# First attention of a hybrid encoder layer: which keys share a transposed tile

## The chip, the cores and the metric

The kernel runs on one core of a Trainium2 chip. The metric is the device time of one execution in microseconds; smaller is better. Its engines are TensorE (PE; PEld is its loading of weights), VectorE (DVE), ScalarE (ACT), GpSimd (POOL) and SyncE (SP, which issues DMAs). Each works off its own queue in order.

## What is computed

One layer of an encoder over 2048 tokens of width 1024, all in float32: a norm and a projection to queries, keys, values and gates, two attentions side by side, a gated merge, and a feed-forward part. The change is in the first attention:

```
windowed_gqa: 8 query heads, 2 key/value heads (4 query heads share one), head width 64
for each block of 128 tokens i:
    keys  = tokens (i-1)*128 .. (i+2)*128          # 384, fewer at the ends
    sc    = q k^T / 8 - slope(head) * |t - s|
    sc    = -inf where |t - s| > 128 or s is no token
    p     = softmax([sc, sink(head)])[..., :-1]
    y     = p v
```

A query attends to the 128 tokens on either side and to itself, so a row of the 384 keys holds 257 that count.

## The kernel before

**The work in order.** The kernel first makes the projection of the first 1024 tokens, then runs the first attention (function `attn_a`, L763), then the second (`attn_b`, L929), both with the rest of the projection between them as dense work, then the gated merge and the feed-forward part. The framework lays out every engine's queue ahead of time: it takes the instructions in the order in which the program issues them as their priority and places each when a simulated timeline says that it can run.

**The dense work.** `feature_tile` (L207) makes 24 products of 512 columns (L203 to L205) from the projection's weights, which GpSimd and ScalarE split into a high and a low part (L179, L180). `paced` (L838) issues such a piece behind the last product of an earlier attention block, at a fixed rate of pieces to blocks, so TensorE has other work to do while a block's softmax runs.

**One block of the first attention.** There are 2 groups of 4 heads and 16 blocks of 128 tokens in each, so 32 calls of `attn_a(g, i)`. The 128 queries are cut into four parts u of 32 tokens; the 128 rows of a tile are 4 heads x 32 tokens. Part u needs the 288 keys from 32u to 32u + 288 of the block's 384.

- First half: a DMA brings the queries, GpSimd reorders them (L774), TensorE multiplies by the keys (L784, two products a part, of high and low parts), VectorE adds distances and takes the maximum (L786), ScalarE the exponentials (L791), VectorE sums and reciprocals (L792, L793), GpSimd scales (L795). The result s is a tile of 128 x 4 x 384 in which what lies outside a part's 288 keys was set to zero once (L753). There are four such tiles, used in turn.
- Second half, for each of the block's key groups c of 128 keys (three; two at the ends): four transposes, one a part, into one bank of 512 columns (L802); ScalarE copies it to `ph` (L805), rounded to the high part; VectorE subtracts that from the bank to get the low part `pl` (L806); two products, v rows by `ph` (L807) and by `pl` (L808), 512 columns each, add up in one bank over all c. A column of v holds the high and the low part of the 64 values side by side, so the bank has 128 rows; L813 and L814 add its two halves, and a DMA stores the result.

The transposes have two banks to use (tag `pt`), the sums have one (`av`), `ph` and `pl` three buffers each.

**What orders the blocks.** `drive` (L828) issues the first half of a block two blocks ahead of the second half of the one that it then finishes. After the last block the pools of the first attention are closed (L885), and those of the second take the same memory (L889, L890): the left ones are piled up from the bottom of a partition, the right ones down from its top. A tile that takes the place of another can be written when the other was used for the last time. The second attention's units are made alike: a query tile for each of three units in turn (`qb0`, `qb1`, `qb2`, loaded at L934), scores (L947), transposes (L975), copies and subtractions (L980, L981), products (L987).

Of the kernel before, what the change touches and what calls it, by code (L numbers as in the profile page):

```python
# [8 lines left out]
F32 = mybir.dt.float32  # L9
F32R = mybir.dt.float32r  # L10
AF = mybir.ActivationFunctionType
ALU = mybir.AluOpType
# [10 lines left out]
P = 128  # L23
# [72 lines left out]
def encoder_layer(ctx, tc, x, norm_mix, w_in, b_gate, sink, rpb, w_pa, w_pb, w_out,  # L96
                  norm_mlp, w_up, w_down, norm_final, dist_a, mask_b, out):
    nc = tc.nc
    V, A, G, PE, SY = nc.vector, nc.scalar, nc.gpsimd, nc.tensor, nc.sync

    def pool(name, side=None, space=None, stack=None):
        kw = {"reuse_waits": "tile"} if space is not DRAM else {}
        if side:
            kw["side"] = side
        if space:
            kw["space"] = space
        return (stack or ctx).enter_context(tc.tile_pool(name=name, bufs=1, **kw))
# [13 lines left out]
    def psum(tag, bufs):  # L121
        n_ps[0] += 1
        return pps[tag].tile([P, 512], F32, tag=tag, bufs=bufs, name=f"{tag}_{n_ps[0]}")
# [3 lines left out]
    def T(pl, shape, dt, tag, bufs):  # L127
        n_t[0] += 1
        pl = pl[tag] if isinstance(pl, dict) else pl
        return pl.tile(shape, dt, tag=tag, bufs=bufs, name=f"{tag}_{n_t[0]}")  # L130


    ident = cp.tile([P, P], F32, name="ident")
# [37 lines left out]
    def put(dst, src):  # L171
        pending.append((dst, src))

    def flush(keep=0, queue=A):
        while len(pending) > keep:
            queue.dma_start(*pending.pop(0))
# [131 lines left out]
    def ring(stack, tag, shape, dt, bufs, side="right"):  # L308

        pl = pool(f"r_{tag}", side=side, stack=stack)  # L310
        return lambda: T(pl, shape, dt, tag, bufs)
# [263 lines left out]
    for p in range(2):  # L575
        t = T(xp, [P, D], F32, "xin", 8).rearrange("p (k c) -> p k c", k=4)
        c = QUADS[2][0]
# [93 lines left out]
    s_h = ExitStack()  # L671
    hpl = [pool(f"hT{n}", side="left", stack=s_h) for n in range(4)]
    s_a = ExitStack()
    ap_ = pools(s_a, "left", ("ka1", "va1", "qraw", "qa", "sta", "sa", "ya", "ph", "pl", "biasa1", "byhead"), "a")
    ap_.update(pools(s_a, "right", ("biasa0", "va0", "ka0"), "a"))
    hp = {}

# [53 lines left out]
    for h in range(4):  # L731
        at = slice(h * A_Q, (h + 1) * A_Q)
# [4 lines left out]
    def make_bias_a(g):  # L737
        t = T(ap_, [P, A_K], F32, f"biasa{g}", 1)
        SY.dma_start(t, dist_a)
        G.tensor_scalar(t, t, slope[:, g : g + 1], 1.0, ALU.mult, ALU.mult)  # L740
        bias_a[g] = t
# [4 lines left out]
    vas = [T(ap_, [P, 16, P], F32R, f"va{g}", 1) for g in range(2)]  # L746
# [8 lines left out]
    def load_kv(g, m, behind=None):  # L755
        k, kd = kas[g][:, :, m * (S // 2) : (m + 1) * (S // 2)], ks_a[m][g]
        with tc.issue_after(behind) if behind else nullcontext():
# [2 lines left out]
            SY.dma_start(k[64:128, 1].bitcast(F32), kd[0:64])  # L760
            SY.dma_start(vas[g][:, 8 * m : 8 * m + 8].bitcast(F32), vs_a[m][g])

    def attn_a(g, i):  # L763
        c0, c1 = (1 if i == 0 else 0), (2 if i == 15 else 3)
        if bias_a[g] is None:

            with tc.issue_after(shares[2]):
                make_bias_a(g)
        base = (i - 1) * P
        by_head = T(ap_, [P, 4, P], F32, "qraw", 3)  # L770
        q = T(ap_, [P, 4, 4, A_Q], F32R, "qa", 2)
        s = sas[len(began) % 4]
        began.append(SY.dma_start(by_head, qs_a[g][i // 8][:, :, i % 8]).ins)
        G.tensor_copy(out=q.rearrange("p u h q -> p h u q"), in_=by_head.rearrange("p h (u q) -> p h u q", u=4))  # L774
        ka, v = kas[g], vas[g]
        st = T(ap_, [P, 8, 4], F32, "sta", 8)
        mx, nm, sm, es, ri = (st[:, k, :] for k in range(5))
        sink_g = sink_p[:, g : g + 1]
        span = [(max(u * A_Q, c0 * P), min(u * A_Q + A_K, c1 * P)) for u in range(4)]
        for u, (lo, hi) in enumerate(span):  # L780
            n = hi - lo
            ps = psum("s", 3)
            for z in range(2):
                PE.matmul(ps[:, :n], q[:, u].rearrange("p h q -> p (h q)"), ka[:, z, base + lo : base + hi],  # L784
                          start=z == 0, stop=z == 1)
            V.tensor_tensor_reduce(out=s[:, u, lo:hi], in0=ps[:, :n], in1=bias_a[g][:, lo - u * A_Q : hi - u * A_Q],  # L786
                                   scale=1.0, scalar=sink_g, op0=ALU.add, op1=ALU.max, accum_out=mx[:, u : u + 1])
        A.activation(nm, mx, AF.Copy, scale=-1.0)
        A.activation(es, mx, AF.Exp, bias=sink_g, scale=-1.0)
        for u, (lo, hi) in enumerate(span):  # L790
            A.activation(s[:, u, lo:hi], s[:, u, lo:hi], AF.Exp, bias=nm[:, u : u + 1], accum_out=sm[:, u : u + 1])  # L791
        V.tensor_tensor(out=sm, in0=sm, in1=es, op=ALU.add)  # L792
        V.reciprocal(ri, sm)  # L793
        for u, (lo, hi) in enumerate(span):
            share = G.tensor_scalar(s[:, u, lo:hi], s[:, u, lo:hi], ri[:, u : u + 1], 1.0, ALU.mult, ALU.mult)  # L795
        shares.append(share.ins)
        yield
        po = psum("av", 1)
        for c in range(c0, c1):
            pt = psum("pt", 2)  # L800
            for u in range(4):
                PE.transpose(pt[:, u * P : (u + 1) * P], s[:, u, c * P : (c + 1) * P], ident)  # L802
            ph = T(ap_, [P, 512], F32R, "ph", 3)
            pl = T(ap_, [P, 512], F32R, "pl", 3)
            A.copy(ph, pt)  # L805
            V.tensor_tensor(out=pl, in0=pt, in1=ph.bitcast(F32), op=ALU.subtract)  # L806
            PE.matmul(po, v[:, i - 1 + c, :], ph, start=c == c0, stop=False)  # L807
            last = PE.matmul(po, v[:, i - 1 + c, :], pl, start=False, stop=c == c1 - 1).ins  # L808
        done.append(last)
        t = T(ap_, [64, 512], F32, "ya", 2)  # L810
        t4 = t.rearrange("d (h u q) -> d h u q", h=4, u=4)
        by_u = po.rearrange("p (u h q) -> p h u q", u=4, h=4)
        A.copy(t4, by_u[64:128])  # L813
        V.tensor_tensor(out=t4, in0=by_u[0:64], in1=t4, op=ALU.add)  # L814
        flush(queue=SY)
        put(y_a[g].rearrange("(h d) t -> d h t", d=64)[:, :, i * P : (i + 1) * P],
            t.rearrange("d (h q) -> d h q", h=4))
# [56 lines left out]
    for g in (1, 0):  # L874
        load_kv(g, 0)
    drive((attn_a(g, i) for g in (1, 0) for i in range(7)), live, False)
    paced(fill, range(12), 24, 3)
    flush(queue=SY)
    for g in range(2):
        load_kv(g, 1, began[8 + 3 * g])  # L880
    drive((attn_a(g, i) for g in range(2) for i in range(7, 16)), live, True)
    paced(fill, range(12, 24), 24, 3)
    del done[:]
# [579 lines left out]
    rows = [ring(s_dn, tag, [P, BT], F32, 8) for tag in "XYZW"]  # L1463
# [120 lines left out]
    for n in (1, 6, 2, 7, 5, 3, 4):  # L1584
        for group in ((range(8),) if n != 4 else (range(4), range(4, 8))):
# [14 lines left out]
            last = []  # L1600
# [55 lines left out]
```

## Time and profile before

| | |
|---|---|
| median of 3 runs | 2606.74 us (2605.96 to 2606.89) |
| the profiled execution | 2605.6 us, span of its instructions 2603.8 us |
| TensorE busy | 2571.4 us, 99% of the span |
| VectorE, ScalarE, GpSimd busy | 1608.0, 1232.4, 368.1 us |
| the first attention | about 376 to 646 us of the span |
| the second attention | about 610 to 1021 us |

A row of a group gives line, engine, operation, the tiles written and read, the shape and the count; then the busy time, the mean duration in ns of one, and the idle time of the engine before them, with what ended it. A row of a timeline gives the start and the duration in us. "SPq" is the queue that issues DMAs. A row of busy times by stretch gives the length of the stretch and then, engine by engine, the busy time and the number of instructions, then TensorE's granted clock, the DMA share and GB/s.

### The profile page before, as it was taken

What the parts mean: (1) busy time and instruction counts of PE and PEld (TensorE: products, weight loads), DVE (VectorE), ACT (ScalarE), POOL (GpSimd) and SP (SyncE); (2) the same over time, 40 slices, a digit from 0 to 9 for tenths busy, and PEclk for the clock granted to TensorE, in tenths of its full rate; (3) what the DMA queues carried; (4) which work ended last, traced back from release to release, by engine and by line L of the source; (5) the groups of instructions that cost most, each with busy time, mean ns of one, the idle gap of its engine ahead of it and who ended that gap; (6) DMA issues with size and microseconds to landing.
All of it is one profiled execution on the core that took longest, in us unless ns stands there. A gap on an engine that the chain in (4) does not pass through costs nothing.

```text
span 2603.8 us, 34627 instructions
## 1 busy us (share of the span) xinstructions
PE 2571.4 (99%) x12140; PEld 2143.3 (82%) x12140; DVE 1608.0 (62%) x2621; ACT 1232.4 (47%) x2261; POOL 368.1 (14%) x493
## 2 busy tenths in 40 slices
PE   8999999999999999999999999999999999999999
PEld 6888788788888888888888888888888888888887
DVE  8865666665544444665478677766656535554766
ACT  5334356666555555542335544644444322323454
POOL 1000124444655541000000000100000000000010
PEclk9999999999999999999999999999999999999999
DMA  5657486465975745865466665854428825445555
GB/s 185 203 155 202 132 260 166 119 167 154 247 212 173 207 140 188 273 202 161 143 198 207 238 222 200 306 173 146 158 100 313 290 97 186 146 148 167 186 193 171
DMA packets 354127, 490.40 MB, mean 188 GB/s; under 512 B 28808, under 2 KB 188808, under 8 KB 351776
## 3 DMA queue, kind: packets, MB, share of 16 engines
q1 hardware_dynamic: 346896, 471.14, 57.6%
q10 hardware_dynamic: 7056, 17.04, 1.8%
q8 instruction: 96, 1.57, 0.2%
q14 instruction: 79, 0.65, 0.1%
HBM read 328.64 MB, written 159.45 MB: 187 GB/s over the span
## 4 chain that ended last, share of the span: by engine, by line
PE 90%; DVE 4%; DMA 2%; ACT 2%; issue 1%; SPq 0%; POOL 0%; DVEq 0%; POOLq 0%; ACTq 0%
PE b L300 15%; PE b L302 15%; PE b L301 15%; PE mm L203 6%; PE mm L205 6%; PE mm L204 6%; PE zb L300 3%; PE zb L302 3%; PE zb L301 3%; PE pt L203 2%; PE pt L204 2%; PE pt L205 2%; PE av L987 2%; PE pt L975 2%; PE s L947 2%; PE pt L802 1%
## 5 line engine op out<-in xcount | busy, mean ns | idle before, releaser
L301 PE MATMUL b<-dwh,dah 128*128 128x512 f32 x896 | 348.5, 389 | 0.0
L302 PE MATMUL b<-dwh,dah 128*128 128x512 f32 x896 | 347.6, 389 | 0.0
L300 PE MATMUL b<-dwh,dah 128*128 128x512 f32 x896 | 339.6, 389 | 0.0
L296 ACT CAST dah<-da 128x1024 fp32r<-128x1024 f32 (+1 forms) x128 | 120.9, 945 | 368.0 <-PE b L302 245.9
L297 DVE TENSOR_TENSOR dah<-da,dah 128x1024 fp32r<-128x1024 f32 (+1 forms) x128 | 139.5, 1090 | 221.3 <-ACT dah L296 216.8
L301 PE MATMUL b<-ubh,uwhlb 128*128 128x512 f32 x592 | 230.3, 389 | 0.0
L300 PE MATMUL b<-ubh,uwhlb 128*128 128x512 f32 x592 | 230.2, 389 | 0.0
L302 PE MATMUL b<-ubh,uwhlb 128*128 128x512 f32 x592 | 229.2, 389 | 0.0
L203 PE MATMUL mm<-hT,whl 128*128 128x512 f32 x544 | 218.6, 402 | 0.0
L205 PE MATMUL mm<-hT,whl 128*128 128x512 f32 x544 | 215.2, 396 | 0.0
L204 PE MATMUL mm<-hT,whl 128*128 128x512 f32 x544 | 214.4, 394 | 0.0
L301 PEld LDWEIGHTS b<-dwh,dah 128*128 128x128 f32 x896 | 168.2, 188 | 35.0
L302 PEld LDWEIGHTS b<-dwh,dah 128*128 128x128 f32 x896 | 168.2, 188 | 34.9
L300 PEld LDWEIGHTS b<-dwh,dah 128*128 128x128 f32 x896 | 168.2, 188 | 34.9
L300 PE MATMUL zb<-zh,zwhl 128*128 128x512 f32 x476 | 186.7, 394 | 8.3 <-DVE zc L293 3.5
L301 PE MATMUL zb<-zh,zwhl 128*128 128x512 f32 x476 | 186.5, 392 | 0.0
L302 PE MATMUL zb<-zh,zwhl 128*128 128x512 f32 x476 | 183.5, 392 | 0.3 <-DVE zwhl L297 0.3
L293 DVE TENSOR_TENSOR uc<-b,uc 128x512 f32<-128x512 f32 x160 | 109.1, 689 | 105.0 <-PE b L302 104.0
L1526 POOL TENSOR_TENSOR st<-st,power 128x1 f32<-128x1 f32 x16 | 13.4, 841 | 925.2 <-DVE st L1525 925.2
L300 PEld LDWEIGHTS b<-ubh,uwhlb 128*128 128x128 f32 x592 | 111.1, 188 | 23.4 <-issue 0.4
L301 PEld LDWEIGHTS b<-ubh,uwhlb 128*128 128x128 f32 x592 | 111.1, 188 | 23.2
L302 PEld LDWEIGHTS b<-ubh,uwhlb 128*128 128x128 f32 x592 | 111.1, 188 | 23.1
(254 smaller groups left out, 5839.3 us busy)
## 6 DMA issues: line engine op xcount, KB each, us to landing
at<-uc SPq DMA_DIRECT2D x224, 256.0 KB
da<-at SPq DMA_DIRECT2D x96, 512.0 KB
dw<-in_w_down_dram SPq DMA_DIRECT2D x160, 256.0 KB
uraw<-in_w_up_dram SPq DMA_DIRECT2D x32, 1024.0 KB
raw<-in_w_in_dram SPq DMA_DIRECT2D x34, 512.0 KB
zraw<-in_w_in_dram SPq DMA_DIRECT2D x16, 1024.0 KB
z<-zg SPq DMA_DIRECT2D x64, 256.0 KB
qraw<-qs_a SPq DMA_DIRECT2D x32, 256.0 KB
```

What stands on the lines that cost most here:

```text
L203: PE.matmul(ps, lh, rh, start=first, stop=False)
L204: PE.matmul(ps, lh, rl, start=False, stop=False)
L205: PE.matmul(ps, ll, rh, start=False, stop=last)
L293: return eng.tensor_tensor(out=out, in0=a, in1=b, op=op).ins
L296: A.copy(hi, src)
L297: return eng.tensor_tensor(out=lo, in0=src, in1=hi.bitcast(F32), op=ALU.subtract).ins
L300: PE.matmul(ps, lh, rh, start=first, stop=False, skip_group_check=True)
L301: PE.matmul(ps, lh, rl, start=False, stop=False, skip_group_check=True)
L302: PE.matmul(ps, ll, rh, start=False, stop=last, skip_group_check=True)
L947: PE.matmul(ps[:, :n], q[:, i, :], kv[:, z, B_R0[i] // 4 : (B_R0[i] + B_NR[i]) // 4, 4 * B_C0[j] : 4 * (B_C0[j] + w)], start=z == 0, stop= ...
L975: PE.transpose(pt[:kp, at + (i - i0) * P : at + (i - i0 + 1) * P], s[i][:, rr : rr + kp], ident)
L987: last = PE.matmul(po[:, i0 * P : (i0 + ni) * P], v[:kp, c, :], src[:kp, o : o + ni * P], start=first, stop=(c == 7 and z == 1), skip_grou ...
```

## The change

The second half of a block takes its keys in another grouping. Of the outer groups c = 0 and c = 2, parts 0 and 1 have all or most of their keys in c = 0 and up to 64 in c = 2, and parts 2 and 3 the other way round.

- `whole` is called twice: for the middle group (c = 1, all four parts), and for the outer ones (c = 0 for parts 0 and 1, c = 2 for parts 2 and 3), four transposes, a copy and a subtraction each. The first gives two products of 512 columns, the second four of 256 (two v row groups, high and low).
- `halved` takes the rests: 64 keys of c = 2 for parts 0 and 1, 64 of c = 0 for parts 2 and 3. Its four transposes have 64 columns of s and give 64 rows. The high part goes to rows 0 to 63 of `ph`, the low part to rows 64 to 127 of the same tile. A product with v rows that are doubled does both at once: two products of 256 columns.
- The doubled rows stand in a new tile `ve` (two buffers). GpSimd fills it in the first half of a block, right behind the reordering of the queries, by up to four copies of 64 rows by 128.
- `halved` is transposed first; its products come last. All products of a block are issued behind all of its transposes.
- `pl` has two buffers in place of three; `ve` is the last pool of the left pile.

A block at the ends has one rest in place of two and half of the outer group.

```diff
-    ap_ = pools(s_a, "left", (..., "ph", "pl", "biasa1", "byhead"), "a")
+    ap_ = pools(s_a, "left", (..., "ph", "pl", "biasa1", "byhead", "ve"), "a")
...
+    def v_rows(g, k, c):
+        return vas[g][64 - 32 * c : 128 - 32 * c, k]
...
         G.tensor_copy(out=q..., in_=by_head...)
+        ve = T(ap_, [P, 2, P], F32R, "ve", 2)
+        for c in (0, 2):
+            if c0 <= c < c1:
+                rows = v_rows(g, i - 1 + c, c)
+                for half in (slice(0, 64), slice(64, P)):
+                    G.tensor_copy(out=ve[half, c // 2], in_=rows)
...
         po = psum("av", 1)
-        for c in range(c0, c1):
+        todo = []
+
+        def whole(keys):
             pt = psum("pt", 2)
-            for u in range(4):
+            for u, c in keys:
                 PE.transpose(pt[:, u * P : (u + 1) * P], s[:, u, c * P : (c + 1) * P], ident)
+            at = slice(keys[0][0] * P, (keys[-1][0] + 1) * P)
             ph = T(ap_, [P, 512], F32R, "ph", 3)
-            pl = T(ap_, [P, 512], F32R, "pl", 3)
-            A.copy(ph, pt)
-            V.tensor_tensor(out=pl, in0=pt, in1=ph.bitcast(F32), op=ALU.subtract)
-            PE.matmul(po, v[:, i - 1 + c, :], ph, start=c == c0, stop=False)
-            last = PE.matmul(po, v[:, i - 1 + c, :], pl, start=False, stop=c == c1 - 1).ins
+            pl = T(ap_, [P, 512], F32R, "pl", 2)
+            A.copy(ph[:, at], pt[:, at])
+            V.tensor_tensor(out=pl[:, at], in0=pt[:, at], in1=ph[:, at].bitcast(F32), op=ALU.subtract)
+            for c in sorted({c for _, c in keys}):
+                us = [u for u, cc in keys if cc == c]
+                cs = slice(us[0] * P, (us[-1] + 1) * P)
+                todo.extend((v[:, i - 1 + c, :], t[:, cs], cs) for t in (ph, pl))
+
+        def halved(cs):
+            pt = psum("pt", 2)
+            ph = T(ap_, [P, 512], F32R, "ph", 3)
+            at = slice(0 if 2 in cs else 256, 512 if 0 in cs else 256)
+            for c in cs:
+                for u in (0, 1) if c == 2 else (2, 3):
+                    k = 2 * P if c == 2 else 64
+                    PE.transpose(pt[0:64, u * P : (u + 1) * P], s[:, u, k : k + 64], ident)
+            A.copy(ph[0:64, at], pt[0:64, at])
+            V.tensor_tensor(out=ph[64:P, at], in0=pt[0:64, at], in1=ph[0:64, at].bitcast(F32), op=ALU.subtract)
+            for c in cs:
+                at = slice(0, 256) if c == 2 else slice(256, 512)
+                todo.append((ve[:, c // 2], ph[:, at], at))
+
+        halved([c for c in (2, 0) if c0 <= c < c1])
+        stacked = todo[:]
+        del todo[:]
+        whole([(u, 1) for u in range(4)])
+        whole([(u, 2 * (u // 2)) for u in range(4) if c0 <= 2 * (u // 2) < c1])
+        todo += stacked
+        for n, (rows, p, at) in enumerate(todo):
+            last = PE.matmul(po[:, at], rows, p, start=n == 0, stop=n == len(todo) - 1, skip_group_check=True).ins
         done.append(last)
```

More of the change, by code (lines that the diff above doesn't have):

```diff
@@ L673, in encoder_layer @@
     s_a = ExitStack()
-    ap_ = pools(s_a, "left", ("ka1", "va1", "qraw", "qa", "sta", "sa", "ya", "ph", "pl", "biasa1", "byhead"), "a")
+    ap_ = pools(s_a, "left", ("ka1", "va1", "qraw", "qa", "sta", "sa", "ya", "ph", "pl", "biasa1", "byhead", "ve"), "a")
     ap_.update(pools(s_a, "right", ("biasa0", "va0", "ka0"), "a"))
```

## The prediction

> **What bounds the kernel now.** I read the page first: the line of engines, then the chain that ended last.
>
> ```profile
> span 2603.8 us, 34627 instructions
> ...
> PE 2571.4 (99%) x12140; PEld 2143.3 (82%) x12140; DVE 1608.0 (62%) x2621; ACT 1232.4 (47%) x2261; POOL 368.1 (14%) x493
> ...
> PE 90%; DVE 4%; DMA 2%; ACT 2%; issue 1%; SPq 0%; POOL 0%; DVEq 0%; POOLq 0%; ACTq 0%
> ```
>
> TensorE is busy for 99% of the span and is 90% of the chain. What shortens its own work counts in full; what shortens another engine's counts only where TensorE waits for it. Next I read the busy times of the first attention's stretch, from the first transpose of L802 to the last product of L808, with the columns PE, PEld, DVE, ACT, POOL.
>
> ```profile
> 376.00:646.00 270.00, 264.21 (x1432) 220.23 (x1431) 166.94 (x475) 179.10 (x497) 124.45 (x191) 1.00 0.58 157
> ```
>
> TensorE stands idle for 5.8 of the 270 us, at the full granted clock (1.00). The others have room: VectorE 62%, ScalarE 66%, GpSimd 46%. The same stretch by groups:
>
> ```profile
> L806 DVE TENSOR_TENSOR pl<-pt,ph 128x512 fp32r<-128x512 f32 x92 | 62.8, 688 | 18.4 <-ACT ph L805 17.9
> ...
> L802 PE MATMUL pt<-ident,sa 128*128 128x128 f32 x368 | 55.9, 272 | 2.5 <-DVE pl L806 2.3 <-DVE sta L793 0.2
> L805 ACT CAST ph<-pt 128x512 fp32r<-128x512 f32 x92 | 53.1, 585 | 51.6 <-PE pt L802 50.8
> ...
> L808 PE MATMUL av<-pl,va 128*128 128x512 f32 x92 | 38.0, 413 | 1.8 <-DVE pl L806 1.4
> L807 PE MATMUL av<-ph,va 128*128 128x512 f32 x92 | 37.9, 412 | 0.3 <-DVE ya L814 0.3
> ...
> L180 POOL TENSOR_TENSOR whl<-raw,whl 128x1024 fp32r<-128x1024 f32 x13 | 31.2, 2396 | 14.5 <-ACT whl L179 12.5 <-PE s L784 1.5 <-PE pt L802 0.6
> ```
>
> The 92 rounds are 28 inner blocks with three key groups and 4 edge blocks with two: 28 x 3 + 4 x 2. Each round is four transposes, a copy, a subtraction and two products 512 wide.
>
> **What one product costs TensorE.** A matmul's duration (412 ns) isn't its price, because matmuls overlap; the step from start to start is. I read it from the timeline of TensorE. The eleven rows left out first are all 512 wide.
>
> ```profile
> 502.19 0.40 PE L204 MATMUL mm<-hT,whl 128*128 128x512 f32 x1
> ...
> 504.96 0.39 PE L204 MATMUL mm<-hT,whl 128*128 128x512 f32 x1
> ...
> 505.92 0.60 PE L802 MATMUL pt<-ident,sa 128*128 128x128 f32 x4
> 506.27 0.48 PE L204 MATMUL mm<-hT,whl 128*128 128x512 f32 x1
> 506.58 0.40 PE L205 MATMUL mm<-hT,whl 128*128 128x512 f32 x1
> ```
>
> Twelve steps in 2.77 us: 0.231 us for 512 columns. From 505.92 to 506.58 stand four transposes and one such product: (0.66 - 0.231) / 4 = 0.107 us for a transpose. Products 256 wide, and transposes of 96 columns, are in the second attention:
>
> ```profile
> 690.59 0.33 PE L987 MATMUL av<-phb,vb 128*128 128x256 f32 x1
> 690.75 0.28 PE L987 MATMUL av<-plb,vb 128*128 128x256 f32 x1
> 690.87 0.28 PE L987 MATMUL av<-phb,vb 128*128 128x256 f32 x1
> 690.99 0.28 PE L987 MATMUL av<-plb,vb 128*128 128x256 f32 x1
> 691.11 0.49 PE L975 MATMUL pt<-ident,sb 128*128 128x128 f32 x3
> ...
> 693.81 0.38 PE L975 MATMUL pt<-ident,sb 128*96 128x128 f32 x2
> ```
>
> Four steps in 0.52 us: 0.13 us each, three of them 0.12. I take 0.13, since in the new order too a change of width comes just before; 0.12 is the other end. Two 96-column transposes end 0.38 us after the first starts; one alone takes 0.27, so the step is 0.11: fewer stationary columns don't shorten it.
>
> **The change, part by part.**
>
> *Products.* An inner block had 6 of 512 columns. It now has 2 of 512 and 6 of 256: four for the outer key groups, whose halves are joined in one tile, and two for the stacked rests, which need no second pass for the low parts. An edge block goes from 4 of 512 to 2 of 512 and 3 of 256. Inner: 4 x 0.231 - 6 x 0.13 = 0.144 us saved; edge: 2 x 0.231 - 3 x 0.13 = 0.072. Sum: 28 x 0.144 + 4 x 0.072 = 4.3 us (6.1 by 0.12). It all lies on the engine that bounds.
>
> *Transposes.* There are 12 and 8 a block, as before, but 4 (edge: 2) have 64 columns, together 120. No row shows 64. Below, the 96-column step says nothing is gained or lost: 0. Above, if each ran alone, it would cost its record, 0.272, in place of 0.107: 120 x 0.165 = 19.8 us. I take 0, since 96 columns is the nearest row.
>
> *Copies and subtractions.* Three of each in an inner block before and after; the stacked pair is 64 partitions by 512 columns, and time doesn't follow partitions: the 64x512 subtraction L814 is as long as L806.
>
> ```profile
> L814 DVE TENSOR_TENSOR ya<-av,ya 64x512 f32<-64x512 f32 x31 | 21.1, 680 | 7.7 <-ACT ya L813 7.5
> ```
>
> An edge block gets a third pair, but two of its three are half as wide: 4 extra instructions on each engine, under 1 us for all, beside TensorE. The gain on these engines is none, whatever becomes of the "two tiles".
>
> *Doubled v rows.* 120 new GpSimd copies of 64 partitions x 128 elements. The nearest rows, one far smaller and one four times as wide:
>
> ```profile
> L774 POOL CAST qa<-qraw 128x512 fp32r<-128x512 f32 x32 | 19.6, 615 | 53.9 <-issue 40.0 <-PE s L784 5.2 <-DMA qraw<-qs_a 3.2
> ...
> L735 POOL COPY byhead<-sink_t 32x2 f32<-32x2 f32 x4 | 0.7, 179 | 0.1
> ```
>
> On the line between them, 128 elements cost 0.179 + 126 x (0.436 / 510) = 0.29 us; ends 0.18 and 0.62. 120 x 0.29 = 35 us (21 to 74), so GpSimd goes from 124 to about 160 of 265 us. Hidden by the dense matmuls that fill TensorE's queue; 1.2 us a block stands in GpSimd's queue behind the cast L774 and ahead of the scalings L795. If the cover is gone, that is rival 2.
>
> *Order.* The stacked rests are transposed first and multiplied last, and all products stand behind all transposes. What stalls TensorE now:
>
> ```profile
> DVE sa L786 <- PE pt L802: 15.9, 15, 3.1
> ...
> PEld av L808 <- DVE pl L806: 5.1, 13, 0.8
> ```
>
> Low-part products wait 5.1 us in 13 of 92 places. Of the new ones only the 32 outer rounds follow their subtraction closely: the middle round's has the outer transposes in between, and the stacked one's both rounds. At best 60 of 92 places go: 3.3 us. At worst none, since the third round needs a bank that the first subtraction must free, as now. I take 1.0, nearer to none.
>
> *Handover.* By the pool lists, the new tile "ve" lies on top of the left pile, where the second attention's second query tile, qb1, comes to lie. Before, qb1 lay on biasa1:
>
> ```profile
> L786 DVE CUSTOM_DVE_ANT_0 sa<-s,biasa,byhead x128: 384/512/540, 371.5 to 607.0; 128x288 f32<-128x288 f32 x112, 128x160 f32<-128x160 f32 x4, 128x192 f32<-128x192 f32 x4, 128x224 f32<-128x224 f32 x4
> ```
>
> ```profile
> 607.89 0.57 SPq L934 DMA_DIRECT2D qb<-qs_b  x1
> ```
>
> ```profile
> 645.91 0.39 PE L808 MATMUL av<-pl,va 128*128 128x512 f32 x1
> ...
> 652.46 1.44 PE L947 MATMUL s<-kb,qb 128*128 128x384 f32 x6
> ```
>
> Its load went out 0.4 us after the last use of that bias. Now it must wait for the last stacked product, which stands where 645.91 stands: 38 us later. What is queued behind it on SP then is the next unit's loads, and the scores of that unit, 8 products, come about as much later. I price this at nothing: the next unit's scores wait until 652.46 anyway, and dense pieces fill the gap. Rival 3 has it otherwise.
>
> *Sum.* -4.3 - 1.0 = -5.3 us, against the profiled execution's 2605.6 (span 2603.8 and 1.8 around it): 2600.3. The median of the runs shown is 1.1 above that execution, so 2606.7 - 5.3 = **2601.4**.
>
> **The rivals.**
>
> [...]
>
> 2. *GpSimd's queue holds the scores back.* Scores now run up to four blocks ahead: L786 waits for L802 (15.9 us above) because there are four score tiles. "ve" has two buffers, so its copies for block n wait for the last product of block n-2, and behind them in GpSimd's queue stand the scalings of n, the cast of n+1 and now and then a weight split (2.4 us, 13 times). The lead shrinks to about two blocks. If TensorE then stalls 1 us at each of 13 splits: -5.3 + 13 = +7.7, **2614.4**. Against it: GpSimd is half idle, and two blocks are 2 x 270 / 32 = 17 us.
>
> 3. *The gain is not passed on.* The chain goes from the first attention into a transfer:
>
> ```profile
> 653.87 10.75 DMA kb<-ks_b
> ```
>
> If the late qb1 or this load sets when the second attention gets going, TensorE idles for what it saved: **2606.7**, give or take 2. Against it: in this stretch TensorE had dense work and hardly waited.
>
> **How the numbers follow.** Forecast 0.45, rival 1 0.25, rival 2 0.15, rival 3 0.15. A measurement of this kernel tells about 0.2%, 5.2 us, from no change. The forecast's own range is 2597 to 2605 (0.12 us products and 3.3 us of stalls gone, to 0.13 with some of the stalls back), so it is faster by more than 5.2 us in 0.27 and within in 0.18. Rival 1, 2606 to 2617 by how much of 0.16 us is laid bare: same 0.10, slower 0.15. Rival 2: same 0.02, slower 0.13. Rival 3: faster 0.01, same 0.11, slower 0.03. Together faster 0.28, same 0.41, slower 0.31. The range 2597 to 2614 leaves out the upper ends of rivals 1 and 2, some 0.13, and 0.03 below; transposes that each run alone would be at the very top of it and beyond.
>
> **What would show it.** Right: L802's steps stay 0.11 with 64 columns; 64 products of 512 and 180 of 256 columns at 0.12 to 0.13; 120 GpSimd copies near 0.29 us; TensorE idle in the stretch at or below 5.8 us; the last product some 5 us before 645.9; everything after it shifted by that. [...] Rival 2: long waits of GpSimd's copy for the products, and TensorE waiting for L795 or L774. Rival 3: an earlier end of the stretch and idle time of TensorE behind it. Wrong would be the whole argument if another stage of the schedule moves: spans before 376 us or after 1016 us that differ by more than a microsecond.

## The result, and the profile after

The changed kernel takes **2618.2 us** (median of 6 runs, 2617.6 to 2619.0), against 2607.2 for the kernel before in the same runs (6 runs, 2606.0 to 2609.0): 1.0042 times as long, with a 95% interval of 1.0032 to 1.0052. It is slower by 11 us. The forecast was 2601.4 us, the range 2597 to 2614.

Three lines from the head of the page of the changed kernel: the span, the engines' busy times, the chain that ended last.

```profile
span 2617.2 us, 34925 instructions
...
PE 2576.6 (98%) x12200; PEld 2150.7 (82%) x12200; DVE 1613.7 (62%) x2625; ACT 1233.4 (47%) x2265; POOL 401.5 (15%) x613
...
PE 92%; DVE 3%; DMA 2%; ACT 1%; issue 1%; SPq 0%; POOL 0%; DVEq 0%; POOLq 0%; ACTq 0%
```

TensorE is *busy* 5.2 us longer (2571.4 before), though it has less to do. That is the first thing to explain. The first attention's stretch, now to its last product at 657.9 us (columns as in the prediction), has TensorE idle for 9.5 us, against 5.8, and the mean granted clock is 0.99, no longer 1.00:

```profile
376.00:657.90 281.90, 272.42 (x1527) 230.02 (x1526) 172.02 (x478) 181.23 (x503) 155.20 (x300) 0.99 0.57 153
```

The groups that the change made, between 376 and 660 us (busy time, mean ns; then the idle time before them):

```profile
L831 PE MATMUL pt<-ident,sa 128*64 128x128 f32 x120 | 19.8, 282 | 0.0
...
L845 PE MATMUL av<-ph,va 128*128 128x512 f32 x32 | 13.7, 430 | 2.2 <-ACT ph L817 1.8
L845 PE MATMUL av<-ph,ve 128*128 128x256 f32 x60 | 12.8, 291 | 0.0
```

TensorE is never idle before the 64-column transposes (L831). What one costs is seen in the timeline of TensorE:

```profile
504.17 0.28 PE L845 MATMUL av<-pl,va 128*128 128x256 f32 x1
504.29 0.27 PE L845 MATMUL av<-ph,va 128*128 128x256 f32 x1
504.40 0.28 PE L845 MATMUL av<-pl,va 128*128 128x256 f32 x1
504.52 0.41 PE L845 MATMUL av<-ph,ve 128*128 128x256 f32 x2
504.76 0.60 PE L813 MATMUL pt<-ident,sa 128*128 128x128 f32 x4
505.12 0.48 PE L203 MATMUL mm<-hT,whl 128*128 128x512 f32 x1
...
511.92 0.60 PE L831 MATMUL pt<-ident,sa 128*64 128x128 f32 x4
512.27 0.52 PE L793 MATMUL s<-ka,qa 128*128 128x288 f32 x2
```

A product of 256 columns is stepped past in 0.12 us (504.17, 504.29, 504.40, 504.52). Four transposes of 64 columns take 0.35 us from the start of the first to the next instruction (511.92 to 512.27), four of 128 columns 0.36 (504.76 to 505.12). Over all groups of four with a score product right behind them, between 360 and 700 us, the median is 0.355 us with 64 columns (17 groups, after) and 0.354 with 128 (21 groups, before); the product ahead is stepped past in 0.23 us and the score product behind in 0.22, with either width. So a switch between the two widths shows no cost.

**Where the time went.** I call "the stretch" what lies between the first dense product (L203, at 360.7 us before) and the last (at 1027.9). In it both attentions run. I add up a fixed step for every TensorE instruction by its width (0.228 us for 512 columns, in proportion for narrower ones, 0.06 for the second attention's products of 128 columns, 0.109 for a transpose): that is its *work*, an estimate from the steps in the timelines. A second part is time at half clock, which I come to below. The rest is what these two leave over: waits above all, most of them too short to show as idle time, since the records of neighbouring products overlap (idle by the records: 7.5 us before, 16.4 after).

| kernel | stretch | work | lost to half clock | rest |
|---|---|---|---|---|
| before | 667.1 | 635.2 | 0 | 31.9 |
| after | 679.6 | 628.4 | 6.8 | 44.4 |

So TensorE's work did fall, by 6.8 us, more than the forecast's 4.3. But 12.5 us more of rest and 6.8 us of half clock came in its place. Outside the stretch the two profiles differ by 0.9 us: 2.7 more ahead of it, of which 1.7 are one spell of half clock at 268 us, and 1.8 less behind it.

**The handover** is the place with the largest waits. SP's queue, the loads of query tiles for the second attention, first two of the kernel before, then those of the changed kernel:

```profile
619.85 0.57 SPq L934 DMA_DIRECT2D qb<-qs_b  x1
624.23 0.57 SPq L934 DMA_DIRECT2D qb<-qs_b  x1
```

```profile
625.94 0.57 SPq L971 DMA_DIRECT2D qb<-qs_b  x1
658.11 0.56 SPq L971 DMA_DIRECT2D qb<-qs_b  x1
659.77 0.56 SPq L971 DMA_DIRECT2D qb<-qs_b  x1
670.49 0.56 SPq L971 DMA_DIRECT2D qb<-qs_b  x1
```

Before, five such loads went out between 600 and 658 us; the one at 607.89 is quoted in the prediction. Now one goes out, at 625.94, and the next only at 658.11, 0.3 us after the last stacked product starts (657.80). What TensorE does then (in brackets: idle before, and what ended it):

```profile
679.59 0.51 PE L984 MATMUL s<-kb,qb 128*128 128x288 f32 x2 [2.63 <-DVE stb L989]
...
686.80 1.05 PE L984 MATMUL s<-kb,qb 128*128 128x384 f32 x4 [2.70 <-DMA qb<-qs_b]
```

It stands still twice for some 2.7 us, once by name for a query tile. Dense pieces did cover the wait at first, up to 672.2 us; then they were used up, and the next one starts at 689.8. The stretch from 675 to 700 us, before and after (columns as in the prediction):

```profile
675.00:700.00 25.00, 25.00 (x146) 22.00 (x145) 15.23 (x35) 16.84 (x36) 14.29 (x15) 1.00 0.84 217
```

```profile
675.00:700.00 25.00, 19.67 (x93) 16.77 (x92) 10.76 (x30) 12.46 (x35) 13.10 (x16) 0.86 1.08 233
```

Before, TensorE had no idle time there; after, it has 5.3 us.

**Half clock.** Stretches of TensorE in the changed kernel; the columns are its length, TensorE's busy time, the granted clock, DMA share and GB/s.

```profile
524.10:527.50 3.40, 2.48 (x12) 1.00 0.73 191
592.30:595.70 3.40, 1.03 (x3) 1.00 0.75 236
677.70:681.10 3.40, 1.51 (x13) 1.00 1.11 324
684.50:687.90 3.40, 1.10 (x6) 1.00 1.19 273
...
527.50:530.90 3.40, 3.40 (x16) 0.50 0.42 108
595.70:599.10 3.40, 3.28 (x14) 0.51 0.24 62
681.10:684.50 3.40, 3.00 (x13) 0.50 1.13 265
687.90:691.30 3.40, 3.40 (x13) 0.50 0.93 157
```

The first four rows are windows of 3.4 us, the last four what came right behind each of them: 3.4 us at half clock. Three of the four windows have TensorE busy for less than half, the one at 524.1 for 2.48 us. All 20 profiles of this study together, after their first 20 us and on the grid on which their spells lie, show no sharp limit: the 30 windows at full clock with at most 1.42 us busy were all followed by half clock, of those between 1.48 and 2.50 us 20 were and 129 were not, and of those above none was. In the changed kernel the starts of the four spells are 20, 25 and 2 times 3.41 us apart, which gives the grid. A spell costs up to 1.7 us, half of its 3.4, and looks *busy*, since the matmuls in it take longer: four transposes of 64 columns are stepped past in 0.71 us (527.86 to 528.57), against 0.35 at full clock, products of 256 columns in 0.21 and 0.22 (528.93, 529.14, 529.36), against 0.12. So busy time can rise while work falls. Before there was none in the stretch, and all six runs of the changed kernel have a lower mean granted clock (0.995 to 0.997) than the profiled execution before (0.999).

Where a wait falls on this grid makes luck part of every run. The kernel before has a wait of 2.0 us up to 488.7 that falls on two windows, and its clock stays whole:

```profile
483.90:487.30 3.40, 2.75 (x17) 1.00 0.79 196
487.30:490.70 3.40, 1.97 (x12) 1.00 0.67 194
490.70:494.10 3.40, 3.40 (x22) 1.00 0.29 66
```

Windows laid otherwise, from 486.0 to 489.4 us, would leave 1.38 us busy in one. In the run with less work, below, such a wait fell mostly into one window (1.39 us busy), and a spell followed. So a few us between two single profiles are nothing; I go by medians and by the work and rest of the stretch.

### The profile page after: what moved, and what is told of

The parts are those of the page before. It is cut to its first block, busy times and chain, and to the rows that moved or that the text cites. A ratio compares the mean times of both kernels' runs of the same rounds, so it can differ in the third digit from the quotient of the medians.

```text
span 2617.2 us, 34925 instructions
## 1 busy us (share of the span) xinstructions
PE 2576.6 (98%) x12200; PEld 2150.7 (82%) x12200; DVE 1613.7 (62%) x2625; ACT 1233.4 (47%) x2265; POOL 401.5 (15%) x613
## 4 chain that ended last, share of the span: by engine, by line
PE 92%; DVE 3%; DMA 2%; ACT 1%; issue 1%; SPq 0%; POOL 0%; DVEq 0%; POOLq 0%; ACTq 0%
PE b L300 15%; PE b L302 15%; PE b L301 15%; PE mm L203 6%; PE mm L204 6%; PE mm L205 6%; PE zb L302 3%; PE zb L300 3%; PE zb L301 3%; PE pt L203 2%; PE pt L204 2%; PE pt L205 2%; PE av L1024 2%; PE pt L1012 2%; PE s L984 2%; PE av L845 1%
## 5 line engine op out<-in xcount | busy, mean ns | idle before, releaser
L203 PE MATMUL mm<-hT,whl 128*128 128x512 f32 x544 | 219.0, 403 | 1.3 <-DVE zc L293 1.3
```

Source lines behind the costliest of these rows:

```text
L203: PE.matmul(ps, lh, rh, start=first, stop=False)
```

## The experiments

All are against the kernel before on the same chip and in the same session, and each run's time is a median; the ratio to the kernel before, with its 95% interval, compares runs of different sessions best. Where it bears on the argument, the four columns of the table above are given as stretch, work, half clock, rest.

**The handover undone.** The changed kernel with "ve" lower in the pile. With `pl` one buffer shorter, everything above `pl` has the address that it had in the kernel before, and `qb1` lies on `biasa1` and its neighbour `byhead` again.

```diff
-    ... "sa", "ya", "ph", "pl", "biasa1", "byhead", "ve"), "a")
+    ... "sa", "ya", "ve", "ph", "pl", "biasa1", "byhead"), "a")
```

> The changed kernel with the tile ve moved down in the pool list, below ph and pl, so that biasa1 lies under the second attention's query tile qb1 again; nothing else differs. Handover theory (the late qb1 costs most): the 6 to 9 us that TensorE idles at 675 to 700 us come back, 2609 to 2612 us, and the load of qb1 goes out near 615 us in place of 658. Theories that put the loss inside the first attention (the order of products, or the two buffers of ve in GpSimd's queue): 2617 to 2619 us.

2610.2 us, ratio 1.0005 (0.9995 to 1.0014): of the 11 us above the kernel before, 1.7 are left. Stretch 669.6, work 628.4, half clock 0, rest 41.2. The next loads go out early again,

```profile
614.57 0.57 SPq L971 DMA_DIRECT2D qb<-qs_b  x1
623.31 0.57 SPq L971 DMA_DIRECT2D qb<-qs_b  x1
628.46 0.56 SPq L971 DMA_DIRECT2D qb<-qs_b  x1
```

and TensorE between 675 and 700 us has no idle time:

```profile
675.00:700.00 25.00, 25.00 (x140) 21.76 (x140) 12.78 (x29) 15.25 (x34) 14.50 (x18) 1.00 0.85 212
```

The address of one tile was worth 9 us by the medians, each against the kernel before of its own session, and 10 in the profiled stretch: 3.2 of rest and 6.8 of half clock. Two of the four spells (at 527.5 and 595.7) lie in the first attention, ahead of the handover, so 3.4 of the 10 may be the luck of that execution: 6 to 10 us is what the two profiles show.

**The handover broken without the change.** The kernel before, with `ya` on top of the pile; `ya` is read until the last block's end, as the stacked products are.

```diff
-    ... "sa", "ya", "ph", "pl", "biasa1", "byhead"), "a")
+    ... "sa", "ph", "pl", "biasa1", "byhead", "ya"), "a")
```

> The kernel before with nothing but its pool list reordered: the result tile ya is last in the left pile, so qb1 lies over a tile that is used until the last block is stored. Handover theory: it loses 6 to 9 us, 2613 to 2616 us, with TensorE waiting for scores of the second attention. The other theories: 2607 us as before, within 1.5.

2624.9 us, ratio 1.0062 (1.0047 to 1.0077). Stretch 686.3, work 635.2, half clock 6.8, rest 44.3. TensorE stands still in one place for 5 us,

```profile
667.35 0.39 PE L205 MATMUL mm<-hT,whl 128*128 128x512 f32 x1
672.74 1.49 PE L947 MATMUL s<-kb,qb 128*128 128x288 f32 x4 [5.00 <-DMA qb<-qs_b]
```

and pays at half clock afterwards. Nothing of the change is in this kernel: the handover alone does it. So the place of a tile is shown to matter from both sides, and here TensorE's long wait names the load. The size was not foreseen: 16 us where 6 to 9 were expected; the loads behind the one at 623.0 went out at 666.6 us, 8 us later than in the changed kernel.

**What is left: the 6.8 us of work don't show.** With the handover mended the kernel is at 2610, 1.7 above the kernel before, and not below it. I first thought of the order of the products, of the place of the copies, and of their buffers.

The products of each round right behind that round, first in the changed kernel, then with "ve" low as well:

```diff
+        whole([(u, 1) for u in range(4)])
+        multiply()
+        whole([(u, 2 * (u // 2)) for u in range(4) if c0 <= 2 * (u // 2) < c1])
+        multiply()
         halved([c for c in (2, 0) if c0 <= c < c1])
+        last = multiply(True)
```

> The changed kernel with each round's products issued right behind that round's copy and subtraction, the middle group first and the stacked rests last in both; pools as in the changed kernel. Theory that products behind all transposes make TensorE wait: waiting before av products falls from about 12 us to 4, 2609 to 2614 us. Handover theory and theory of GpSimd's queue: 2617 to 2619 us.

> The changed kernel with both earlier edits: ve below ph and pl, and each round's products right behind the round. If the two effects are apart, 8 and 3 us come off: 2606 to 2609 us. If the interleaving had gained only by an earlier end of the first attention, which the low ve already gives: 2610 us.

2615.0 (1.0027, 1.0016 to 1.0038) and 2610.4 (1.0011, 1.0001 to 1.0020). Without the mended handover this takes back some 3 us, between what the two theories gave, and in its profile by half clock alone (0 in place of 6.8; rest 46.6). With the mended handover it takes back nothing: rest 41.7, half clock 1.7. The order of the products isn't what takes the gain.

The copies issued in a block's second half:

> The changed kernel with the copies of the doubled v rows issued in the second half of a block, not in the first, so that they no longer stand ahead of the scalings and wait for a product two blocks back; pools as in the changed kernel. Theory of GpSimd's queue: GpSimd's wait for products (25 us) goes and TensorE's stalls in the first attention fall from 28 us towards 18, 2608 to 2613 us. Theory of the products' order and handover theory: 2616 to 2619 us.

2618.0 (1.0038, 1.0023 to 1.0053): nothing. It doesn't test the wait either: GpSimd still waits 24.5 us for products ahead of the copies (25.4 in the changed kernel).

Four buffers of "ve"; then two, with four of `ph` and three of `pl`. Both have "ve" low, and need `qa` higher up, between `pl` and `biasa1`.

```diff
-        ve = T(ap_, [P, 2, P], F32R, "ve", 2)
+        ve = T(ap_, [P, 2, P], F32R, "ve", 4)
```

> The changed kernel with ve low in the pile and four buffers of it in place of two (qa moves to the top of the pile so that qb1 stays early). Theory of GpSimd's queue, that its wait for products two blocks back (18 us with ve low) stalls TensorE: the wait goes, 2603 to 2606 us. Otherwise: 2609 to 2611 us, as with ve low and two buffers.

> The changed kernel with ve low, four buffers of ph and three of pl in place of three and two (qa on top as well). Theory that too few tiles hold back the next block's copies, since three high parts are held until a block's last product: TensorE's waits before av products and transposes fall from 15 us to 9, 2602 to 2606 us. Otherwise: 2609 to 2611 us.

2610.3 (1.0011, 1.0002 to 1.0021) and 2608.8 (1.0000, 0.9990 to 1.0009). Rest 40.0 and 39.1: more buffers buy 1 to 2 us of rest, and nothing in the time that the intervals could tell. The second is the fastest version of the whole change, and it equals the kernel before.

**Are GpSimd's copies to blame?** The kernel before with the 120 copies, which nobody reads, twice: with `qa` high and three `pl`, and with every address above `pl` kept and two `pl`. Between them stands the control: the kernel before with `qa` high.

```diff
+        ve = T(ap_, [P, 2, P], F32R, "ve", 2)
+        for c in (0, 2):
...
+                    G.tensor_copy(out=ve[half, c // 2], in_=rows)
```

> The kernel before with only the 120 copies of doubled v rows added on GpSimd; nothing multiplies them, so they wait for nothing. The tile ve and the query tile qa are placed so that the second attention's tiles come free as early as before. Theory that the copies themselves cost (GpSimd's 33 us more): 2611 to 2614 us. Theory that the loss within the first attention comes from the order and the tiles of the second half of a block: 2607 to 2609 us, no change.

> The kernel before, with nothing changed but the place of qa in the pile of the first attention: above pl instead of below sta. The control for the run of the copies alone, which had moved it. If the place of qa made that run slow (its memory comes free late): the first score of the first attention about 10 us after the first dense piece in place of 3.2, and 5 to 10 us above before. If the copies made it slow, as theory 'GpSimd' has it: the first score at 3 to 4 us after the first dense piece, and within 2 us of before.

> The kernel before, with the 120 copies added and nothing else: rounds of four transposes and products 512 wide as before; nobody reads the doubled rows. The tile of doubled rows lies between ya and ph, pl has two buffers in place of three, and every other tile keeps the address it has before, qa too; so what made the earlier run of the copies alone start its scores 10 us after the first dense piece is gone. Theory 'GpSimd' (the copies in its queue take what the narrower products save): 6 to 10 us above before, the stretch from the first dense piece to the last (667.1 us before) at 673 to 677. Theory 'regrouping' (the waits of the new order of transposes and products take it): within 2 us of before, the stretch at 667 to 669. Two pl buffers in place of three would show as waits of the subtraction for the low-part products.

2618.3 (1.0041, 1.0026 to 1.0056), 2609.8 (1.0008, 0.9998 to 1.0017) and 2618.3 (1.0043, 1.0028 to 1.0058). The place of `qa` costs little; the copies seem to cost 10 us, more than the theory of the copies gave for either run. But look at GpSimd's copies between 360 and 400 us, first in the last of these kernels, then in the changed one with "ve" low:

```profile
L780 POOL CAST ve<-va 64x128 fp32r<-64x128 f32 x48 | 14.0, 292 | 2.3
```

```profile
L783 POOL CAST ve<-va 64x128 fp32r<-64x128 f32 x10 | 2.9, 291 | 0.5
```

A tile that nobody reads comes free at once, so the framework lays 48 copies into these 40 us, where the first blocks begin, and not 10. These two runs measured another thing than the change does. So I took the copies away instead, and doubled them, in the changed order. Without copies, the stacked products take the whole v tile as weights (so the result of those half groups is another), and every address is that of before; with 240, "ve" is low.

```diff
-            todo.append((ve[:, c // 2], ph[:, at], at))
+            todo.append((v[:, i - 1 + c, :], ph[:, at], at))
```

> The changed kernel without doubled rows and without their tile; the stacked products take the whole 128-row v tile as weights instead, so the number, shapes and order of transposes, copies, subtractions and products are those of the changed kernel, and GpSimd does what it does before; the result of the outer half groups is not the reference's. Three pl buffers, and every tile at the address it has before. Theory 'GpSimd': the 6.8 us of TensorE work saved now show: 2600 to 2603, the stretch from the first dense piece to the last at 660 to 662. Theory 'regrouping': still at 2606 to 2610, the stretch at 666 to 670, with TensorE waiting for copies and subtractions as in the first experiment.

> The changed kernel with the doubled rows' tile in the low place (as in the first experiment), and each of the 120 copies issued twice: 240, some 35 us more on GpSimd. Theory 'GpSimd': it costs about as much again as the first set, 5 to 10 us over the first experiment's 2610.2, so 2615 to 2620, with longer waits of TensorE for scores, and the stretch from the first dense piece to the last at 675 to 680 against 669.6. Theory 'regrouping': 2610 to 2612, the stretch at 669 to 671.

Without copies: 2610.5 (1.0013, 1.0003 to 1.0023), stretch 671.5, work 628.4, half clock 1.7, rest 41.4. That is no better than with them (669.6), so the 120 copies cost nothing that these runs can tell, as predicted; and the theory that GpSimd takes the gain falls. With 240: 2633.3 (1.0099, 1.0084 to 1.0114), rest 61.4. The second set costs 23 us where the first was free, more than either theory gave (2620 at most): GpSimd had room for one set and not for two.

**Only in some stretches?** In these kernels the waits lie between the dense pieces. From the first dense product to the last product of the first attention, where dense products follow one another within 4 us, rest and half clock take some 3 us in each of these three kernels: before, after and without copies. By contrast, in the seven to nine gaps of over 4 us without one (71 us in all before, 74 without copies) they take 14.5 us before and 23.5 without copies, 1.7 of it half clock. TensorE's idle times in one such gap of the kernel without copies, and in the same gap of the kernel before:

```profile
591.30 0.49 PE L839 MATMUL av<-ph,va 128*128 128x512 f32 x1 [1.16 <-ACT ph L811]
593.18 1.35 PE L787 MATMUL s<-ka,qa 128*128 128x288 f32 x6 [1.39 <-POOL qa L777]
```

```profile
588.79 0.53 PE L784 MATMUL s<-ka,qa 128*128 128x288 f32 x2 [0.46 <-DVE ya L814]
...
590.73 0.50 PE L808 MATMUL av<-pl,va 128*128 128x512 f32 x1 [0.17 <-DVE pl L806]
```

So I regrouped only the 19 blocks that stand mostly beside dense products, and then only the other 13, both without copies; and the 19 with doubled rows, once with "ve" low and two `pl`, once with `qa` high and three.

```diff
+        stacked_rests = len(began) not in (0, 1, 2, 5, 9, 12, 13, 17, 18, 21, 22, 25, 26)
...
+        if stacked_rests:
+            halved([c for c in (2, 0) if c0 <= c < c1])
...
+        else:
+            for c in range(c0, c1):
```

> The new grouping in 19 of the 32 blocks: those whose transposes and products stand mostly beside dense matmuls. The 13 blocks that stand mostly in stretches of 4 us or more without a dense matmul (by order 0, 1, 2, 5, 9, 12, 13, 17, 18, 21, 22, 25, 26) keep the old one. No doubled rows and no copies (the stacked products take the whole v tile as weights, so the result of those half groups isn't the reference's), every tile where it is before; so it is to be held against the kernel before and the run without copies (stretch from the first to the last dense piece 667.1 and 671.5 us). Theory 'bare stretches' (the saved work is real, and what takes it back is the longer chain of transposes, copies and products where no dense matmul fills in): the saving of 16 inner and 3 edge blocks shows, some 4 us: the stretch at 662 to 664.5, the time 2602 to 2605, and no more than 15.5 us lost in stretches without dense matmuls (14.5 before, 23.5 with the new grouping everywhere). Theory 'regrouping anywhere' (each regrouped block loses about as much as it saves, wherever it stands): 19/32 of the 4.4 us that the run without copies is longer: the stretch at 669 to 671, the time at 2608 to 2611.

> The complement: the new grouping in those 13 blocks alone, the old one in the other 19; again without copies (the same part of the result isn't the reference's), every tile where it is before. Theory 'bare stretches': the loss of the run without copies comes back, less the saving of the others: the stretch from the first dense piece to the last at 671 to 675 (667.1 before), the time at 2610 to 2615, 21 us or more lost in stretches without dense matmuls. Theory 'regrouping anywhere': 13/32 of 4.4 us: the stretch at 668 to 670, the time at 2607.5 to 2610.

> The same 19 blocks regrouped, now with doubled rows and their copies in those blocks, the tile of doubled rows in the low place, pl two buffers. Theory 'bare stretches', with copies that cost little as long as two buffers hold them back: like the run of the 19 blocks without copies, the stretch at 662 to 666, the time at 2602 to 2607. If two pl buffers are too few for the blocks in the old form, that shows as waits of the subtraction for low-part products, and 2 to 4 us more. Theory 'GpSimd': 2609 to 2613, since the copies of the 19 blocks run in the bare stretches before them.

> As the run before, but with three pl buffers, which needs qa above pl: the control with only qa moved had the stretch at 669.1 us, 2.0 above before. Theory 'bare stretches': 2 us above the run without copies: the stretch at 664 to 668, the time at 2604 to 2609. Theory 'GpSimd': 2611 to 2615.

The 19 blocks: 2608.6 (1.0006, 0.9996 to 1.0015), stretch 667.8, work 631.1, half clock 0, rest 36.7, with 16.9 us in the gaps. The 13: 2613.6 (1.0027, 1.0017 to 1.0038), stretch 674.7, work 632.4, half clock 1.7, rest 40.6, with 23.8 in the gaps. With doubled rows: 2609.7 (1.0009, 0.9999 to 1.0018) and 2611.8 (1.0020, 1.0011 to 1.0029). Regrouping in the gaps does cost 7.6 us of stretch and brings back the loss there, as "bare stretches" has it. But regrouping beside dense products gains nothing either: 4.1 us less work, 4.8 us more rest. Half of that rest, 2.4 us, lies in the gaps and about as much in the second attention; beside the dense products of the first attention it stays at some 3 us. Neither theory gives both numbers. The two runs with doubled rows came out where theory "GpSimd" had them, but they don't speak for it: the first is 1.1 us from the same blocks without copies, and the profile of the second holds two spells of half clock (3.4 us; rest 39.5).

**Does saved work count at all?** The last two runs regroup nothing. The kernel before, without the low-part product of c = 0 in the 30 blocks that have one (6.9 us of work less, and the low parts of that group missing from the result), and with that product made twice (as much more, and counted double).

```diff
+            if c > 0:
+                last = PE.matmul(po, v[:, i - 1 + c, :], pl, start=False, stop=c == c1 - 1).ins
```

> The kernel before, with nothing regrouped: only the low-part product of the first outer key group (c = 0) is left out in the 30 blocks that have it, so the low parts of those probabilities are missing from the result. 30 products of 512 columns at 0.23 us: 6.9 us less work on TensorE, as much as the regrouping saves. All copies, subtractions, transposes and their order stay. Theory 'regrouping costs' (TensorE's work counts in full here, and what takes it back is the longer chain that the new grouping makes): the stretch from the first dense piece to the last at 659.5 to 662 us (666.9 before), the time 5 to 8 us below before. Theory 'work is not what bounds' (where no dense matmul fills in, the copies and subtractions set the pace, and TensorE waits for whatever it saves): a third or less of it shows, the stretch at 664.5 to 668, the time within 3 us of before.

> The opposite: the kernel before, with the same 30 low-part products made twice (their low parts count double in the result): 6.9 us more work on TensorE, all else as before. Theory 'regrouping costs': 5 to 8 us above before, the stretch at 672 to 674.5 us. Theory 'work is not what bounds': the added work takes the place of waits in the stretches without dense matmuls, but costs in full beside dense ones: 2 to 5 us above before, the stretch at 669 to 672.

Less: **2606.0**, ratio 0.9994 (0.9985 to 1.0002), 1.1 us below before, which is not to be told from no change (by the interval, at most 4 us are gained); stretch 666.2, work 628.4, half clock 1.7, rest 36.1. More: **2616.0**, ratio 1.0029 (1.0019 to 1.0039), 8.8 above (7.6 by the ratio); stretch 677.7, work 642.0, half clock 1.7, rest 34.0. The waits of TensorE (its weight loads are PEld) between 360 and 660 us tell where it went; in us, times, longest. Before:

```profile
PEld s L784 <- DVE sta L786: 2.1, 6, 0.5
...
PE s L784 <- DVE sta L786: 0.5, 2, 0.3
```

With less work:

```profile
PEld s L784 <- DVE sta L786: 4.3, 10, 0.6
...
PE s L784 <- DVE sta L786: 1.4, 5, 0.4
...
PE s L784 <- POOL qa L774: 1.0, 1, 1.0
```

TensorE comes to the next scores sooner and waits there for VectorE to have read the last ones: 4.1 us more in these rows, some of it at the same time on PE and PEld; the rest has grown by 4.2. One window of this kernel is more than half empty, and the clock drops behind it (columns as for the windows above). Where the wait falls on the grid has its part in that; without this spell the stretch would be 2.6 us shorter than before, not 0.9:

```profile
485.50:488.90 3.40, 1.39 (x12) 1.00 0.83 246
488.90:492.30 3.40, 3.39 (x12) 0.51 0.42 97
```

The expectation "work is not what bounds" holds for less work, and "regrouping costs" is refuted there; for more work both gave too little. In this stretch the kernel before stands near a balance: 6.9 us of TensorE's work more cost 8.8 (a spell of half clock, which its profile shows, may be 1.7 of that), and 6.9 less gain 1.

What stays open: why the regrouped kernel without copies is 5 us worse in the stretch than this one (671.5 against 666.2) at the same work and with one spell each. Its rest is 5.3 us more, mostly in the gaps. The chain within a block is one guess; but the framework lays out all queues anew for every kernel, and no run holds that layout fixed.

## Why the prediction was wrong, point by point

The measured time is 16.8 us above the forecast, and two steps make up most of it: the handover, some 9 us by the medians, and a gain of 5.3 that didn't come. The first is shown by moving one tile, the second by taking work away in the old order.

- **"It all lies on the engine that bounds."** This step failed. The price of the products was right but for its choice of 0.13 us a step (0.12, the other end that the text named, was measured), so the work fell by even more than forecast. But a busy share of 99% was taken to mean that each us saved counts. The run with less work shows that about 1 us of 6.9 does, and that the rest grows by 4.2 in its place. The page's 5.8 us of idle TensorE in the stretch was read as little room for waits; with less work the waits were there.
- **"I price this at nothing: the next unit's scores wait until 652.46 anyway, and dense pieces fill the gap."** This step failed too, and it is the larger one: it cost some 9 us. The load's delay was right (38 us forecast; 607.89 to 658.11 is 50, of which 12 are the later end of the stage). But one unit of the second attention was scaled before the first one ended, where it had been two, and the dense pieces filled the gap only up to 672.2 us, with TensorE idle for 5.3 us between 675 and 700. A smaller slip stands in the reading of the kernel before: its load at 607.89 followed, by 0.02 us, the last read of `byhead`, the tile above `biasa1` (L789, 607.59 to 607.87), and not that of the bias.
- **Stalls, −1.0.** Wrong in sign. Weight loads of products now wait for ScalarE's copy, too (3.7 us in 7 places), and those for low parts rose from 5.1 us to 6.6; TensorE's idle time in the stretch went from 5.8 to 9.5.
- **64-column transposes, 0.** Right: 0.35 us for four, beside 0.36. Rival 1 falls: no run shows any of the 0.16 us a switch that its times rest on; the product ahead is stepped past in 0.23 us and the score product behind in 0.22, with 64 columns as with 128.
- **Doubled rows.** 289 ns each, against 0.29 us forecast, and hidden, as the runs with and without them show. Rival 2's sign was there (the copy waits 25.4 us for products), but the kernel without copies is no faster.
- **Rival 3** came closest: a late `qb1` set when the second attention gets going. It gave 2606.7, because it let TensorE lose only what it had saved. Here the late transfer took more than that, in waits and in half clock.
- **A slower kernel** had a chance of 0.31, 0.28 of it for rivals 1 and 2. It came from an address and from saved work that didn't count.
- **"Wrong would be the whole argument if another stage of the schedule moves."** Ahead of 360 us the two profiles differ by 2.7 us, more than the one allowed; but 1.7 of that is a spell of half clock, and over all 20 profiles the first dense product starts anywhere from 360.7 to 364.6 us. That is within the scatter.

## What to carry to other kernels

When a new tile is put into a pool, look up what the next stage lays on that address and when the tile is read for the last time; put what is read last where it is needed last. A busy share of 99% didn't say here that saved work counts: take the same amount of work away, and add it, in the old order, before building a new one. And a control that leaves out a tile's readers also leaves out what holds its writers back.

## What the runs showed of the hardware

- A 3.4 us window with TensorE busy for at most 1.42 us was followed by 3.4 us at half clock in all 30 cases of 20 profiles, one of 1.48 to 2.50 us in 20 of 149, a fuller one never: up to 1.7 us on top of the wait. Where a wait falls on the grid has its part in it: a wait of 2.0 us spread over two windows, 2.75 and 1.97 us busy, left the clock at 1.00.
- FP32 transposes with 64 stationary columns among 128-column products cost here what those with 128 do: 0.35 and 0.36 us for four.
- 120 GpSimd copies of 64 x 128 (289 ns each) cost this kernel nothing that could be measured, 120 more cost 23 us.
